# Multiplying C by the scan's running state in three rounded passes, with one more lane step before the state's update (bidirectional SSD encoder, one core)

## The chip, the cores and the metric

The kernel runs on one core of a Trainium2 chip. The metric is device microseconds of one execution, and the kernel before took 1793.29 us, the median of three runs between 1792.80 and 1793.42 us. One more execution was taken with the profiler on; its time and span are in the table below. The profile names the engines PE (matrix multiply), PEld (the load of a matmul's stationary operand), DVE (VectorE), ACT (ScalarE), POOL (GpSimd) and SP (SyncE, which issues the DMAs here).

## The reference

One layer of an encoder is applied to two sequences, a sample of 1024 tokens and a prompt of 256: a normalised row is multiplied by `w_in`, the result goes through three groups of heads (a bidirectional SSD scan, windowed attention, attention to a memory of 256 rows), and the three outputs are multiplied by `w_out` and added to the input. The change lies in the scan. For each chunk of 128 tokens and each direction it is:

```
acs     = cumsum(dt * A)
y_diag  = (C B^T * decay) xdt                  # inside the chunk
states  = B^T (xdt * exp(acs_end - acs))       # what the chunk adds to the state
S_next  = exp(acs_end) * S + states            # running state, 128 x (heads x 64)
y_off   = (C S) * exp(acs)                     # what earlier chunks give: the product of the change
```

Everything is float32.

## The kernel before

**Tiles and blocks.** The 1280 tokens are ten tiles of 128 (`NT`); tiles 0 to 7 are the sample and 8 and 9 the prompt, and they are also two groups of five tiles (640 tokens). The big products run block by block, a block being some columns of a weight: `block_tok` (L234) has tokens as its stationary operand and 512 columns as the moving one, `block_feat` (L269) the other way around, and `block_pair` (L1183) does the first and the last part with sums of weights and rows. Each block runs over the 16 parts k of the inner dimension. A weight is split by `wsplit` (L204) into a rounded high part `h` (ACT copy into float32r, L206) and a remainder `l` (DVE subtraction, L207), the rows are split in the same way, and each product is three passes: high by high, high by low, low by high (L258 to L260, L293 to L295, L1235 to L1237).

**Lanes.** All else (scan, attention, preparation) is written as generators that stand in two queues, `lanes`. Lane 0 has the attention, lane 1 has `dt_prep`, `ssd_up` and `ssd_down`. After each k of a block, `pump` adds the two numbers of `RATES` for that block to what each lane is owed and runs that many steps, alternating between the lanes; a step is the code between two `yield`s. `need` runs a lane on until a named piece is done, at points where a later block reads its result, and in the third `w_out` block, at k = 9, both lanes are emptied at once before their memory is closed. This order is the order of priority; the tile framework places the instructions of each engine from it when the kernel is built, with what it takes to be ready first, and the weight splits are given a higher priority.

**The scan.** `ssd_up(t)` (from L806) goes through the tiles upwards. It turns B and x (L823, L824, L860), and then, for each half g of the 16 heads (512 columns of the running `state`, a 128 x 1024 tile), it multiplies x by the decays and splits the results (`xf`, `fh`, `fl` forward, `xb`, `bh`, `bl` backward), multiplies C by the state (`pyf`, L884, a plain float32 matmul of 128 x 512), scales that into `ya` (L885), multiplies B by the split x in three passes (`pst`, L867 to L869, in `into`), updates the state (L905, L906), and stores the backward contribution `st` (L915, L916). `ssd_down(t)` (from L1014) goes downwards with the stored contributions: `pyb` (L1062) is C by the state, `y` is put together from it (L1064 to L1066), squared (L1069), and then the state is updated (L1071, L1072). Tiles 0 and 8 are `first` and tiles 7 and 9 `last`; `pyf` is made where a tile is not first and `pyb` where it is not last, each for two halves.

**Buffers.** Small tiles come from rings: tag `wb` has four slots of 128 x 512 (`WBB`), tag `bc` and tags `btok` and `btl` one each. The lanes' products go to three PSUM banks (`psum`, tag `mix`), the blocks' sums to five others.

Of the kernel before, what the change touches and what calls it, by code (L numbers as in the profile page):

```python
# [10 lines left out]
F32 = mybir.dt.float32  # L11
F32R = mybir.dt.float32r
# [3 lines left out]
AF = mybir.ActivationFunctionType  # L16
# [3 lines left out]
P = 128  # L20
# [9 lines left out]
RBB = 4  # L30

RATES = ({'kv': (4.0, 1.0), 'z1': (2.2, 1.7)},
         {'kv': (1.4, 1.5), 'x': (2.1, 2.15), 'q': (2.2, 2.5), 'za': (2.1, 2.5), 'z0': (2.1, 2.5),
          'z1': (2.05, 2.55), 'mq': (1.95, 2.7), 'zm': (1.75, 2.75), 'o': (2.1, 2.4)})
FAR = 1e30

UNITS = (0, 8, 1, 9, 2, 10, 3, 11, 4, 12, 5, 13, 6, 7)
# [7 lines left out]
def hymba_encoder_kernel(  # L45
# [7 lines left out]
    V, A, G, T, S = nc.vector, nc.scalar, nc.gpsimd, nc.tensor, nc.sync  # L53
# [72 lines left out]
    def hv(ap, n=8):  # L126
        return ap.rearrange("p (h d) -> p h d", h=n)

    def hb(ap, n, d):
        return ap.unsqueeze(2).broadcast_to([P, n, d])  # L130
# [672 lines left out]
    def wb(name, dtype=F32, shape=(P, 512)):  # L803
        return mp.tile(list(shape), dtype, tag="wb", name=name, bufs=WBB)

    def ssd_up(t):  # L806
        first = t in (0, NS)
        last = t in (NS - 1, NT - 1)
# [12 lines left out]
        ps = psum("pcb")  # L821
# [24 lines left out]
        def rows(q):  # L846

            rf = mp.tile([P, 512], F32, tag="rf", name="rf", bufs=2)
            mt = mp.tile([P, 512], F32, tag="rb", name="rb", bufs=RBB)
            r0 = 32 * (t % 5) + 4 * q  # L850
            for d, r in enumerate((rf, mt)):
                S.dma_start(r, ac_d[t // 5][r0 + 16 * d:r0 + 16 * d + 4, :]
                            .rearrange("h c -> (h c)").partition_broadcast(P))
            rows_[q] = rf, mt

        xsT = []
        for g in range(2):
            ps = psum("pxs")
            for j in range(4):
                T.transpose(ps[:, j * P:(j + 1) * P].bitcast(F32R), xc[g][:, j, :], identr)  # L860
            xt = mp.tile([P, 512], F32, tag="xs", name="xs", bufs=2)
            V.tensor_copy(xt, ps)
            xsT.append(xt)
            yield
        def into(ps, g, h, l):

            T.matmul(ps, bth[:, g, :], h, start=True, stop=False)  # L867
            T.matmul(ps, bth[:, g, :], l, start=False, stop=False)
            T.matmul(ps, btl[:, g, :], h, start=False, stop=True)  # L869

        ya = []
        for g in range(2):
            c = slice(g * 512, (g + 1) * 512)
            a = mp.tile([P, 512], F32, tag="ya", name="ya", bufs=2)
            ya.append(a)
            rows(g)
            if not last:
                xf = wb("xf")
                V.tensor_mul(hv(xf), hv(xsT[g]), hb(dd_all[:, (t + 1) % 6, 8 * g:8 * g + 8], 8, 64))
                fh = wb("fh", F32R)  # L880
                A.activation(fh, xf, AF.Copy)
            if not first:
                pf = psum("pyf")
                T.matmul(pf, bc[:, 2 + g, :], state[:, c], start=True, stop=True)  # L884
                V.tensor_mul(hv(a), hv(pf), hb(eacs_all[:, t, 8 * g:8 * g + 8], 8, 64))  # L885
            yield
            if not last:
                fl = wb("fl", F32R)
                V.tensor_sub(fl, xf, fh.bitcast(F32))
            if not first:  # L890
                xb = wb("xb")
                V.tensor_mul(hv(xb), hv(xsT[g]), hb(dd_all[:, (t + 1) % 6, 16 + 8 * g:24 + 8 * g], 8, 64))
                bh = wb("bh", F32R)
                A.activation(bh, xb, AF.Copy)
            yield
            if not last:
                ps = psum("pst")
                into(ps, g, fh, fl)
                if t == 0 and g == 0:

                    need(mk_prep, range(4))
                if first:
                    V.tensor_copy(state[:, c], ps)
                else:
                    V.tensor_mul(hv(state[:, c]), hv(state[:, c]), hb(cd_all[:, t, 8 * g:8 * g + 8], 8, 64))  # L905
                    V.tensor_add(state[:, c], state[:, c], ps)  # L906
                yield
            if not first:
                bl = wb("bl", F32R)
                V.tensor_sub(bl, xb, bh.bitcast(F32))  # L910
                yield
                ps = psum("pst")
                into(ps, g, bh, bl)
                st = wb("st")
                A.activation(st, ps, AF.Copy)  # L915
                S.dma_start(sb_d[t][:, c], st)  # L916
                yield
# [77 lines left out]
    def norm_ssd():  # L995

        if "y" in last_y:
            t, ys, rs = last_y.pop("y")
            for g in range(2):
                V.tensor_scalar(out=ys[g], in0=ys[g], scalar1=rs[:, g:g + 1], scalar2=None, op0=ALU.mult)  # L1000
                last_y[g] = t, ys[g]
# [12 lines left out]
    def ssd_down(t):  # L1014
        first = t in (0, NS)
        last = t in (NS - 1, NT - 1)
        tok = slice(t * P, (t + 1) * P)
        ss = sm.tile([P, 2], F32, tag="s2", name="yss", bufs=4)
        if not last:
            cc = mp.tile([P, 2, P], F32, tag="btok", name="cc", bufs=1)  # L1020
            S.dma_start(cc, xbc_d[10:12, :, tok].rearrange("f p c -> p f c"))
        ld = []
        for g in range(2):
            c = slice(g * 512, (g + 1) * 512)

            y = mp.tile([P, 512], F32, tag="ya" if t % 2 else "rf", name="yd", bufs=2)
            S.dma_start(y, yp_d[t][:, c])
            if g == 0 and t < 5:
                z = mp.tile([P, 512], F32R, tag="xs", name="zd", bufs=2)
                S.dma_start(hv(z.bitcast(F32), 4), yT_d[:, :, tok])  # L1030
            else:
                z = mp.tile([P, 512], F32, tag="xs", name="zd", bufs=2)
                S.dma_start(z, z_d[g][t])
            st = None
            if not first:
                st = state[:, c] if last else wb("st2")
                S.dma_start(st, sb_d[t][:, c])
            d = mp.tile([P, 4, P], F32R, tag="rb", name="ydT", bufs=RBB)
            S.dma_start(d.bitcast(F32), yd_d[t][:, 4 * g:4 * g + 4, :])
            ld.append((y, z, st, d))  # L1040

        def diag_in(g):
            ps = psum("pd")
            for j in range(4):
                T.transpose(ps[:, j * P:(j + 1) * P].bitcast(F32R), ld[g][3][:, j, :], identr)
            V.tensor_add(ld[g][0], ld[g][0], ps)

        for _ in range(9 if last else 4):
            yield
        norm_ssd()  # L1050
        diag_in(0)
        yield
        for g in range(2):
            c = slice(g * 512, (g + 1) * 512)
            y, z, st, _ = ld[g]
            if g == 0 and t < 5:
                zr, z = z, psum("pz")
                for j in range(4):
                    T.transpose(z[:, j * P:(j + 1) * P].bitcast(F32R), zr[:, j * P:(j + 1) * P], identr)
            if not last:  # L1060
                pf = psum("pyb")
                T.matmul(pf, cc[:, g, :], state[:, c], start=True, stop=True)  # L1062
                y2 = wb("y3")
                V.tensor_mul(hv(y2), hv(pf), hb(eacs_all[:, t, 16 + 8 * g:24 + 8 * g], 8, 64))  # L1064
                V.tensor_add(y, y, y2)
            V.tensor_mul(y, y, z)  # L1066
            if g == 0 and t < 5:
                z = wb("zq")
            A.activation(z, y, AF.Square, scale=0.5, accum_out=ss[:, g:g + 1])  # L1069
            if not first and not last:  # L1070
                V.tensor_mul(hv(state[:, c]), hv(state[:, c]), hb(cd_all[:, t, 16 + 8 * g:24 + 8 * g], 8, 64))  # L1071
                V.tensor_add(state[:, c], state[:, c], st)  # L1072
            yield
            turn_ssd(g)
            if g == 0:
                diag_in(1)
                yield
        rs = sm.tile([P, 2], F32, tag="s2", name="yrs", bufs=4)
        rsqrt(rs, ss, 1.0 / 512, 2)
        G.tensor_scalar(out=rs, in0=rs, scalar1=0.5, scalar2=None, op0=ALU.mult)  # L1080
        last_y["y"] = t, [x[0] for x in ld], rs
        yield
        if first:
            for _ in range(3):
                yield
            norm_ssd()
            yield
            yield
            for g in range(2):
                turn_ssd(g)  # L1090
                yield
# [636 lines left out]
```

## Time and profile before

| | |
|---|---|
| median of three runs | 1793.29 us (1792.80 to 1793.42) |
| the profiled execution: its own time | 1792.72 us |
| the profiled execution: span from first to last instruction | 1791.0 us |
| granted clock of TensorE | 1.000 |
| instructions in the span | 31429 |

The time of an execution is the span and some 1.7 us around it. Stages of the span, from the trace: up to about 580 us the memory block, the first group's blocks in pairs and the preparation; from about 580 to 1200 us the blocks in which `ssd_up` and the attention run beside the second group's products; from 1200 to 1500 us those with `ssd_down`; then the last blocks of `w_out`. A matmul's record has a length that reaches beyond the start of the next one, since matmuls are pipelined: what one costs is read from the distance of starts, not from its length. A matmul whose operands are float32 shows as two records, each with a weight load; one whose operands are float32r shows as one.

### The profile page before, as it was taken

What the parts mean: (1) busy time and instruction counts of PE and PEld (TensorE: products, weight loads), DVE (VectorE), ACT (ScalarE), POOL (GpSimd) and SP (SyncE); (2) the same over time, 40 slices, a digit from 0 to 9 for tenths busy, and PEclk for the clock granted to TensorE, in tenths of its full rate; (3) what the DMA queues carried; (4) which work ended last, traced back from release to release, by engine and by line L of the source; (5) the groups of instructions that cost most, each with busy time, mean ns of one, the idle gap of its engine ahead of it and who ended that gap; (6) DMA issues with size and microseconds to landing.
All of it is one profiled execution on the core that took longest, in us unless ns stands there. A gap on an engine that the chain in (4) does not pass through costs nothing.

```text
span 1791.0 us, 31429 instructions
## 1 busy us (share of the span) xinstructions
PE 1777.5 (99%) x10838; PEld 1605.0 (90%) x10838; DVE 1248.7 (70%) x2358; ACT 922.2 (51%) x2049; POOL 549.6 (31%) x900
## 2 busy tenths in 40 slices
PE   9999999999999999999999999999999999999999
PEld 7789999999998999999889977877988888899999
DVE  5595788888868877778766575557777644766665
ACT  6554555554434766656465565544447533543332
POOL 0105789998810101001001000000100000057775
PEclk9999999999999999999999999999999999999999
DMA  8653444445446644453635645557777754744442
GB/s 292 199 180 114 144 148 149 144 142 163 123 145 207 188 142 137 136 162 111 193 111 179 182 149 162 165 160 249 233 224 238 240 185 149 223 149 144 148 142 77
DMA packets 208207, 301.12 MB, mean 168 GB/s; under 512 B 19568, under 2 KB 86192, under 8 KB 208048
## 3 DMA queue, kind: packets, MB, share of 16 engines
q1 hardware_dynamic: 207904, 299.06, 54.3%
q8 instruction: 85, 1.39, 0.3%
q14 instruction: 74, 0.61, 0.1%
q10 hardware_dynamic: 144, 0.06, 0.0%
HBM read 236.36 MB, written 62.69 MB: 167 GB/s over the span
## 4 chain that ended last, share of the span: by engine, by line
PE 71%; issue 7%; POOL 7%; DVE 6%; DMA 6%; ACT 3%; SPq 0%; POOLq 0%; ACTq 0%; DVEq 0%
PE acc L258 8%; PE acc L260 8%; PE acc L259 8%; PE acc L293 5%; PE acc L1237 5%; PE acc L295 5%; PE acc L294 5%; PE acc L1235 5%; PE acc L1236 5%; POOL ws L1207 4%; PE accm L1236 2%; PE accm L1235 2%; PE accm L1237 2%; POOL wraw L1207 2%; PE po L673 1%
## 5 line engine op out<-in xcount | busy, mean ns | idle before, releaser
L207 DVE TENSOR_TENSOR wl<-wraw,wh 128x512 fp32r<-128x512 f32 (+1 forms) x480 | 345.3, 721 | 220.0 <-ACT wh L206 199.8
L206 ACT ACTIVATE wh<-wraw 128x512 fp32r<-128x512 f32 (+1 forms) x480 | 292.1, 613 | 305.8 <-PE acc L260 154.1
L258 PE MATMUL acc<-wh,xH 128*128 128x512 f32 (+1 forms) x1088 | 418.4, 385 | 0.5 <-ACT mkr L420 0.3
L260 PE MATMUL acc<-wh,xL 128*128 128x512 f32 (+1 forms) x1088 | 411.2, 378 | 0.0
L259 PE MATMUL acc<-wl,xH 128*128 128x512 f32 (+1 forms) x1088 | 410.4, 377 | 0.7 <-DVE wl L207 0.7
L258 PEld LDWEIGHTS acc<-wh,xH 128*128 128x128 f32 x1088 | 204.5, 188 | 38.7 <-issue 3.6
L259 PEld LDWEIGHTS acc<-wl,xH 128*128 128x128 f32 x1088 | 204.6, 188 | 38.2 <-DVE wl L207 3.3
L260 PEld LDWEIGHTS acc<-wh,xL 128*128 128x128 f32 x1088 | 204.4, 188 | 36.8 <-issue 0.6
L293 PE MATMUL acc<-xH,wh 128*128 128x320 f32 x640 | 202.9, 317 | 0.5 <-DVE zs L309 0.5
L206 ACT ACTIVATE sh<-ws 128x384 fp32r<-128x384 f32 x176 | 91.4, 523 | 214.0 <-POOL ws L1207 117.0
L294 PE MATMUL acc<-xL,wh 128*128 128x320 f32 x640 | 199.2, 311 | 0.0
L295 PE MATMUL acc<-xH,wl 128*128 128x320 f32 x640 | 198.3, 310 | 0.0
L207 DVE TENSOR_TENSOR sl<-ws,sh 128x384 fp32r<-128x384 f32 x176 | 124.1, 708 | 105.1 <-ACT sh L206 104.9
L1207 POOL TENSOR_TENSOR ws<-wraw 128x128 f32<-128x128 f32 x176 | 113.5, 645 | 204.5 <-DMA wraw<-in_w_in_pairs_dram 81.1
L635 POOL COPY lg<-nsink 128x2 f32<-128x2 f32 x40 | 16.4, 410 | 373.9 <-PE ppt L663 239.6
L293 PEld LDWEIGHTS acc<-xH,wh 128*128 128x128 f32 x640 | 120.3, 188 | 3.3 <-issue 2.2
L294 PEld LDWEIGHTS acc<-xL,wh 128*128 128x128 f32 x640 | 120.3, 188 | 2.0 <-issue 1.7
L295 PEld LDWEIGHTS acc<-xH,wl 128*128 128x128 f32 x640 | 120.2, 188 | 0.8 <-issue 0.7
L1207 POOL TENSOR_TENSOR ws<-wraw,ws 128x128 f32<-128x128 f32 x176 | 116.6, 662 | 13.8
L1207 POOL TENSOR_TENSOR wraw<-wraw 128x128 f32<-128x128 f32 x176 | 112.2, 638 | 13.7
L1207 POOL TENSOR_TENSOR ws<-ws,wraw 128x128 f32<-128x128 f32 x176 | 115.0, 653 | 0.0
L362 DVE SCALAR_TENSOR_TENSOR c<-u,vec,c 128x638 f32<-128x638 f32 (+1 forms) x96 | 89.7, 936 | 8.9 <-ACT c L357 8.6
(437 smaller groups left out, 3947.0 us busy)
## 6 DMA issues: line engine op xcount, KB each, us to landing
wraw<-in_w_in_laid_dram SPq DMA_DIRECT2D x176, 256.0 KB, 2.9
wraw<-in_w_in_pairs_dram SPq DMA_DIRECT2D x112, 256.0 KB, 2.7
wraw<-in_w_out_laid_dram SPq DMA_DIRECT2D x64, 256.0 KB, 3.0
wraw<-in_w_out_pairs_dram SPq DMA_DIRECT2D x64, 256.0 KB, 2.9
rf<-ac SPq DMA_DIRECT2D x40, 256.0 KB, 4.0
rb<-ac SPq DMA_DIRECT2D x40, 256.0 KB, 4.9
wraw<-in_w_mem_laid_dram SPq DMA_DIRECT2D x32, 256.0 KB, 4.8
xst<-in_x_sample_dram SPq DMA_DIRECT2D x20, 256.0 KB, 4.9
```

The source lines that it names most:

```text
L206: a = A.activation(h, raw, AF.Copy)
L207: b = V.tensor_sub(l, raw, h.bitcast(F32))
L258: T.matmul(ps[t][:, :n], sh, h[:, :n], start=(k_ == 0), stop=False)
L259: T.matmul(ps[t][:, :n], sh, l[:, :n], start=False, stop=False)
L260: T.matmul(ps[t][:, :n], sl, h[:, :n], start=False, stop=(k_ == KT - 1))
L293: T.matmul(o, sh, cur["H", q][:, m, c], start=(k == 0), stop=False)
L294: T.matmul(o, sh, cur["L", q][:, m, c], start=False, stop=False)
L295: T.matmul(o, sl, cur["H", q][:, m, c], start=False, stop=(k == KT - 1))
L1207: G.tensor_tensor(out=o, in0=x, in1=y, op=op)
L1235: T.matmul(ps[p], h, xh, start=(k_ == 0), stop=False)
L1236: T.matmul(ps[p], h, xl, start=False, stop=False)
L1237: T.matmul(ps[p], l, xh, start=False, stop=(k_ == 7))
```

## The change

In `ssd_up`, C (the last two rows of `bc`) is split once for each tile into a high part and a remainder, in place of B, which is no longer needed then. For each half, the state's 512 columns are split into `sh` (ACT) and `sl` (DVE), in two slots of `wb`, in the step in which `xf` and `fh` are made; the product follows a step later, in three float32r passes (`by_state`), with its scaling. Where a tile is neither first nor last, one more `yield` stands before `into`, the product with B that ends in the update of the state. In `ssd_down`, C is split into `cch` and `ccr` (slots `btl` and `btok`), the state's halves into slots of `bc` and `wb`: the first half a step before its product, the second in the step before its own. There the state's update now stands directly behind the product and ahead of the product's scaling, and the square goes into the slot of `y2` instead of a slot of its own. Eight of the lane rates are changed.

```diff
-         {'kv': (1.4, 1.5), 'x': (2.1, 2.15), 'q': (2.2, 2.5), 'za': (2.1, 2.5), 'z0': (2.1, 2.5),
-          'z1': (2.05, 2.55), 'mq': (1.95, 2.7), 'zm': (1.75, 2.75), 'o': (2.1, 2.4)})
+         {'kv': (1.4, 1.5), 'x': (2.1, 2.2), 'q': (2.2, 2.6), 'za': (2.1, 2.65), 'z0': (2.05, 2.65),
+          'z1': (2.0, 2.65), 'mq': (1.95, 2.8), 'zm': (1.75, 2.8), 'o': (2.1, 2.4)})
...
+    def by_state(ps, ch, cl_, h, l):
+
+        T.matmul(ps, ch, h, start=True, stop=False)
+        T.matmul(ps, ch, l, start=False, stop=False)
+        T.matmul(ps, cl_, h, start=False, stop=True)
+
     def ssd_up(t):
...
+        if not first:
+            A.activation(bcr[:, 0:2], bc[:, 2:4], AF.Copy)
+            V.tensor_sub(bcr[:, 2:4], bc[:, 2:4], bc[:, 0:2])
+
         def into(ps, g, h, l):
...
             rows(g)
+            if not first:
+                sh, sl = wb("sh", F32R), wb("sl", F32R)
+                A.activation(sh, state[:, c], AF.Copy)
+                V.tensor_sub(sl, state[:, c], sh.bitcast(F32))
             if not last:
                 xf = wb("xf")
                 V.tensor_mul(hv(xf), hv(xsT[g]), hb(dd_all[:, (t + 1) % 6, 8 * g:8 * g + 8], 8, 64))
                 fh = wb("fh", F32R)
                 A.activation(fh, xf, AF.Copy)
+            yield
             if not first:
                 pf = psum("pyf")
-                T.matmul(pf, bc[:, 2 + g, :], state[:, c], start=True, stop=True)
+                by_state(pf, bcr[:, g, :], bcr[:, 2 + g, :], sh, sl)
                 V.tensor_mul(hv(a), hv(pf), hb(eacs_all[:, t, 8 * g:8 * g + 8], 8, 64))
-            yield
             if not last:
                 fl = wb("fl", F32R)
                 V.tensor_sub(fl, xf, fh.bitcast(F32))
...
             yield
+            if not first and not last:
+                yield
             if not last:
                 ps = psum("pst")
                 into(ps, g, fh, fl)
...
         if not last:
-            cc = mp.tile([P, 2, P], F32, tag="btok", name="cc", bufs=1)
+            ccr = mp.tile([P, 2, P], F32R, tag="btok", name="cc", bufs=1)
+            cc = ccr.bitcast(F32)
             S.dma_start(cc, xbc_d[10:12, :, tok].rearrange("f p c -> p f c"))
...
         norm_ssd()
+        parts = {}
+
+        def halves(g):
+            if last:
+                return
+            c = slice(g * 512, (g + 1) * 512)
+            h = mp.tile([P, 512], F32R, tag="bc", name="sh", bufs=1)
+            l = wb("sl", F32R)
+            A.activation(h, state[:, c], AF.Copy)
+            V.tensor_sub(l, state[:, c], h.bitcast(F32))
+            parts[g] = h, l
+
+        if not last:
+            cch = mp.tile([P, 2, P], F32R, tag="btl", name="cch", bufs=1)
+            A.activation(cch, cc, AF.Copy)
+            V.tensor_sub(ccr, cc, cch.bitcast(F32))
+        halves(0)
         diag_in(0)
         yield
...
             if not last:
                 pf = psum("pyb")
-                T.matmul(pf, cc[:, g, :], state[:, c], start=True, stop=True)
+                by_state(pf, cch[:, g, :], ccr[:, g, :], *parts.pop(g))
+                if not first:
+                    V.tensor_mul(hv(state[:, c]), hv(state[:, c]), hb(cd_all[:, t, 16 + 8 * g:24 + 8 * g], 8, 64))
+                    V.tensor_add(state[:, c], state[:, c], st)
                 y2 = wb("y3")
                 V.tensor_mul(hv(y2), hv(pf), hb(eacs_all[:, t, 16 + 8 * g:24 + 8 * g], 8, 64))
                 V.tensor_add(y, y, y2)
             V.tensor_mul(y, y, z)
             if g == 0 and t < 5:
-                z = wb("zq")
+                z = y2
             A.activation(z, y, AF.Square, scale=0.5, accum_out=ss[:, g:g + 1])
-            if not first and not last:
-                V.tensor_mul(hv(state[:, c]), hv(state[:, c]), hb(cd_all[:, t, 16 + 8 * g:24 + 8 * g], 8, 64))
-                V.tensor_add(state[:, c], state[:, c], st)
             yield
             turn_ssd(g)
             if g == 0:
+                halves(1)
                 diag_in(1)
                 yield
```

## The prediction

> **What bounds the kernel now.** I read the page from the top: busy times, the slices, then the chain that ended last.
>
> ```profile
> span 1791.0 us, 31429 instructions
> PE 1777.5 (99%) x10838; PEld 1605.0 (90%) x10838; DVE 1248.7 (70%) x2358; ACT 922.2 (51%) x2049; POOL 549.6 (31%) x900
> PE   9999999999999999999999999999999999999999
> DVE  5595788888868877778766575557777644766665
> PEclk9999999999999999999999999999999999999999
> PE 71%; issue 7%; POOL 7%; DVE 6%; DMA 6%; ACT 3%; SPq 0%; POOLq 0%; ACTq 0%; DVEq 0%
> ```
>
> TensorE has work in every slice, at full clock, and is without a record for 1791.0 − 1777.5 = 13.5 us. A busy PE need not be an efficient one, so I then asked whom PE waits for, the longest waits first:
>
> ```profile
> PE pmt L767 <- DVE mpr L759: 2.0, 3, 1.1
> PE pyb L1062 <- ACT so L1011: 1.1, 1, 1.1
> PE psc L641 <- DVE nm L643: 0.9, 1, 0.9
> PE acc L259 <- DVE wl L207: 0.7, 3, 0.2
> PE pst L868 <- DVE fl L889: 0.2, 1, 0.2
> ```
>
> No wait of PE is longer than a few us in sum: whatever the lanes do, the instructions placed behind them keep PE fed. So the kernel lasts as long as its matmuls take one after the other, and a change is worth what it takes from that row of matmuls or adds to it, plus new waits in it. The stages of the change, by windows, leave room elsewhere:
>
> ```profile
> 580.00:1200.00 620.00, 616.34 (x3908) 544.83 (x3907) 429.60 (x957) 369.12 (x930) 54.74 (x90) 1.00 0.51 156
> 1200.00:1500.00 300.00, 297.08 (x1700) 249.88 (x1699) 194.16 (x390) 145.54 (x344) 23.25 (x43) 1.00 0.70 218
> ```
>
> The columns after the length are PE, PEld, DVE, ACT and POOL: DVE is busy 69% and 65% of the two stages, ACT 60% and 49%.
>
> **The change part by part.** *The products.* The two old ones, by line, and PE's timeline around one of them, and around a product that already goes in three passes:
>
> ```profile
> L884 PE MATMUL pyf<-state,bc x32: 591/592/697, 645.2 to 1418.9; 128*128 128x512 f32 x32
> L1062 PE MATMUL pyb<-state,cc x32: 590/593/697, 1203.0 to 1500.1; 128*128 128x512 f32 x32
> 645.20 1.02 PE L884 MATMUL pyf<-state,bc 128*128 128x512 f32 x2
> 646.05 0.60 PE L663 MATMUL ppt<-identr,lg 128*128 128x128 f32 x4
> 648.36 0.40 PE L867 MATMUL pst<-fh,bth 128*128 128x512 f32 x1
> 648.59 0.40 PE L868 MATMUL pst<-fl,bth 128*128 128x512 f32 x1
> 648.82 0.39 PE L869 MATMUL pst<-fh,btl 128*128 128x512 f32 x1
> 649.05 0.31 PE L294 MATMUL acc<-xL,wh 128*128 128x320 f32 x1
> ```
>
> Each line has 32 records, two to a product: 16 products in `ssd_up` (tiles 1 to 7 and 9, two halves) and 16 in `ssd_down`, 32 in all. The records' lengths (0.59 us) overlap and say little; the starts say what a product costs: from 645.20 to the next matmul at 646.05 it is 0.85 us in plain float32. Three float32r passes of the same 128x512 shape start 0.23 us apart and give PE on from 648.36 to 649.05, 0.69 us. `by_state` has that shape and that type, so each product becomes 0.16 us shorter, and 32 of them take 32 × 0.16 = 5.1 us out of the row of matmuls. PE has nothing to hide this in, so it counts in full.
>
> A page weighs in here. The Trainium skill (FP8 and Floating Point Precision, TensorE Precision Notes) says that true FP32 is four passes through the array. By that an old product would take 4 × 0.23 = 0.92 us and the gain be 32 × 0.23 = 7.4 us; the trace has 0.85 us, 3.7 passes, and I go by the trace.
>
> *The splits.* Each product now needs its half of the state copied by ACT and subtracted by DVE, and each tile its C. Rows of the same kinds:
>
> ```profile
> L881 ACT ACTIVATE fh<-xf 128x512 fp32r<-128x512 f32 x16 | 10.0, 626 | 13.7 <-DVE xf L879 11.1 <-DMA rb<-ac 2.6
> L889 DVE TENSOR_TENSOR fl<-xf,fh 128x512 fp32r<-128x512 f32 x16 | 11.0, 689 | 5.1 <-ACT fh L881 5.0
> L617 ACT ACTIVATE qh<-q 128x256 fp32r<-128x256 f32 x20 | 7.8, 408 | 8.2 <-DVE q L611 8.2
> L618 DVE TENSOR_TENSOR qh<-q,qh 128x256 fp32r<-128x256 f32 x20 | 8.1, 419 | 1.0 <-ACT qh L617 1.0
> ```
>
> ACT gets 32 × 0.626 + 16 × 0.408 = 26.6 us, DVE 32 × 0.689 + 16 × 0.419 = 28.7 us. In the two stages DVE goes from 429.6 + 194.2 = 624 to 653 of 920 us, 71%, and ACT from 515 to 541. What hides them is the block's matmuls on PE; if that cover were gone, one split would cost its full 0.626 + 0.689 = 1.3 us, 42 us for all 32.
>
> *The new wait.* The product now waits for `sl`, which is made one lane step earlier. Behind it on PE stand the block's matmuls, and for those wait the block's evacuations and all else. No row shows this wait, but `pst` has the same one, for `fl`, and over its 32 products it cost PE 0.2 us in one place (above). The bounds are 0 (PE is handed a product only when it is ready) and 42 us (each split exposed); I take 0.2 us, the row that is like it in every respect but the lane's distance.
>
> *More work on DVE and ACT.* PE's waits for DVE and ACT in the rows above come to 4.9 us. If they grow as DVE's work in these stages does, 28.7 / 624 = 4.6%, that is 0.2 us; some rows are not shown, so I put 0.4. Bounds: a loss of as much again as the waits that are there, 5 us, and a gain of the 1.1 us at `pyb`, since other instructions will stand before it.
>
> *The state's update ahead of the scaling.* In `ssd_down`, for the 12 halves that have an update, two DVE instructions now stand ahead of the one that reads `pf`:
>
> ```profile
> L1071 DVE TENSOR_TENSOR state<-state,cd_all x12: 680/681/685, 1205.0 to 1308.8; 128x512 f32<-128x512 f32 x12
> L1072 DVE TENSOR_TENSOR state<-state,st x12: 681/686/690, 1206.2 to 1310.0; 128x512 f32<-128x512 f32 x12
>   ACT so L1011: 2.8, 3
> ```
>
> They need the halves split, not the product, so they can run before PE is done, and then cost nothing. At worst they hold one of three PSUM banks 0.681 + 0.686 = 1.37 us longer; the last row is what `pyb` waited for in its old place, mostly such a bank (2.8 us in three places, by the view of its line, which counts the weight load's waits too). I take 0.
>
> *Lane steps and rates.* One `yield` more for each half of tiles 1 to 6 makes 12 more steps of lane 1; from its yields, `ssd_up(2)` goes from 36 steps to 38. Counting both kernels' steps against their rates, block by block, the pieces end where they did within some k: `ssd_up(7)` at k = 14 of block z1 instead of 13, `ssd_down(7)` starts at k = 0 of mq in both, `ssd_down(0)`, which a later block needs, ends at k = 1 of the first `w_out` block in both, and when the lanes are emptied 3 steps are left instead of 5. No `need` forces a step in either. So I cost this at 0; what hides it is the distance from `ssd_down(0)` to its reader, one whole block, and if that were used up, `w_out` would wait. No DMA is added, and SP's and POOL's queues keep their order. Using `y2` for the square frees a slot and adds no wait, since the square waits for `y` anyway.
>
> *The sum.* −5.1 + 0.2 + 0.4 = −4.5 us. The profiled execution took 1792.72 us (its span and 1.7 us around it) and becomes 1788.2; it is 0.57 us below the median, so by the median the forecast is 1793.3 − 4.5 = **1788.8 us**, 0.25% faster. About 0.2%, 3.6 us, is what a measurement of this kernel can tell from no change, so faster begins below 1789.7 us.
>
> **The rivals.** *The bank takes it back.* If the banks are held 1.37 us longer in 12 places and PE waits for it in as many as it now waits for `so`, 3 of them, 4.1 us are lost: −4.5 + 4.1, so 1792.9 us, no change that can be told. For it speaks that three banks serve all lane products; against it that the update can run ahead of the product.
>
> *The ring of four.* This one ends on the other side. In `ssd_up`, `sh` and `sl` are drawn from `wb` ahead of `xf` and `fh`, four slots at once, and for the second half one of the four still holds the `st` of the first half, on its way out to memory:
>
> ```profile
> sb<-st SPq DMA_DIRECT2D x16, 256.0 KB, 3.3
> ```
>
> Before, only `xf` and `fh` were drawn at that point. If `fh` has to wait for the landing, 3.3 us, less the 0.63 + 0.69 us of the split ahead of it, ACT stands 2.0 us with the block's weight splits queued behind it, in six places (tiles 1 to 6). If all of it came through to PE it would be 6 × 2.0 = 12 us, hence 1788.8 + 12.0 = 1800.8 us. It makes the kernel slower (by over 0.2%) from 8.1 / 6 = 1.35 us a place. Against it: the weights are split ahead of their use (`wl` held PE only 0.7 us), and a framework that knows of the slot can put other ACT work first.
>
> *More than the bare passes.* If the 1.1 us of `pyb` and the 2.0 us that PE waits at `pmt` go in the new order, 1788.8 − 3.1 = 1785.7 us. The new order may also move such waits instead.
>
> *The weight loads are the bound.* A product has three loads instead of two, 32 more:
>
> ```profile
> L884 PEld LDWEIGHTS pyf<-state,bc x32: 186/189/193, 645.1 to 1418.5; 128*128 128x128 f32 x32
> 642.85 0.19 PEld L293 LDWEIGHTS acc<-xH,wh 128*128 128x128 f32 x1
> 643.00 0.19 PEld L294 LDWEIGHTS acc<-xL,wh 128*128 128x128 f32 x1
> ```
>
> If PE's time went with their number, 32 × 0.189 = 6.0 us would be added and the kernel take 1793.3 + 6.0 = 1799.3 us. But loads of 0.19 us start 0.15 us apart, beside matmuls, and three of them lie within the 0.69 us of a `pst`: they are hidden. The Trainium skill (Perfetto Trace Analysis, Identifying the Most-Contended Engine) says that matmul busy time is a bad measure of headroom and that the share of LDWEIGHTS is the good one. By that rule this change, which raises the share, goes the wrong way; the trace speaks against it here, and I leave it a small chance.
>
> *It does not do what it says.* If float32r passes from these tiles ran at the plain float32 pace, three would cost more, not less; every float32r row here is at 0.23 us, so this has no chance of its own.
>
> **How the numbers follow.** The forecast has 0.47, the bank 0.25, the ring 0.16, more than the passes 0.10, the loads 0.02. The forecast's own range is 1787.0 to 1790.5 us (the waits from 0 to some 2 us more, the passes measured to 0.01 us each), and nine tenths of it, 0.42, lie below 1789.7. Faster: 0.42 + 0.10 = 0.52. Same: 0.05 + 0.25 = 0.30. Slower: 0.16 + 0.02 = 0.18. The range leaves out the ring and the loads, and so reaches from 1785.0, below the case of more than the passes, to 1794.0, above the bank's 1792.9.
>
> **What would show it.** In the changed trace `by_state` has 96 records, 0.23 us apart, 0.69 us to the next matmul; if the distance is over 0.8, the first step is wrong. PE's waits for `sl` and `ccr` stay under 1 us; several us there mean that the split is too late. DVE rises by about 29 and ACT by about 27 us. A wait of ACT `fh` for the store of `st`, with later `wh` behind it, would show the ring, and more or longer waits at `pyb`, `pd`, `psc` or `pmt` the bank. What would make the forecast wrong is most of all the order of instructions: it is worked out anew for the changed kernel, and moves PE's few us of waits by as much as the gain.

## The result, and the profile after

The changed kernel takes 1797.86 us (median of ten runs, 1795.73 to 1800.88) beside 1793.34 us of the kernel before (ten runs, 1790.97 to 1794.36): 0.27% slower, ratio 1.0027 with a 95% interval of 1.0018 to 1.0036. The forecast was 1788.8 us. The profiled execution took 1795.89 us, 3.2 us more than the one of before, so it shows some two thirds of the difference.

The page after, its span and its busy times:

```profile
span 1794.2 us, 31591 instructions
PE 1775.1 (99%) x10870; PEld 1611.3 (90%) x10870; DVE 1272.5 (71%) x2406; ACT 943.4 (53%) x2097; POOL 554.4 (31%) x900
```

PE is busy 2.4 us less, yet the span is 3.2 us longer: its time without a record went from 13.5 to 19.1 us. So PE got less to do and lost more than that by waiting. First the part that came as forecast, PE's timeline of the changed kernel around one of the new products:

```profile
644.86 0.48 PE L808 MATMUL pyf<-sh,bc 128*128 128x512 f32 x1
645.18 0.40 PE L809 MATMUL pyf<-sl,bc 128*128 128x512 f32 x1
645.41 0.39 PE L810 MATMUL pyf<-sh,bc 128*128 128x512 f32 x1
645.64 0.28 PE L641 MATMUL psc<-kT,qT 128*128 128x256 f32 x1
```

From the second pass on they stand 0.23 us apart. The first record is long (0.48 us) because it starts inside the transposes before it; what a matmul costs is the distance of its end from the end of the one before, for the third pass here 645.80 − 645.58 = 0.22 us. The median of these distances over all records is 0.43 us for each of the two records of an old product, 0.859 us in all, and 0.23 us for a pass, 0.697 us for three. For 32 products that is 5.2 us less work for PE, where the forecast had 5.1. If each of the 10838 (now 10870) records is put down at the median of its kind (same target, same shape), the sum goes from 1761 to 1756 us. What the distances exceed these medians by went from 24 to 32 us.

Then the waits of PE, longest first (total, times, longest):

```profile
PE pxs L866 <- ACT mpr L754: 2.1, 1, 2.1
PE acc L259 <- DVE wl L207: 1.8, 4, 1.1
PE psc L641 <- ACT qT L625: 1.7, 2, 1.5
PE warm L1546 <- DVE zero L1544: 1.3, 1, 1.3
PE acc L258 <- DVE zs L319: 1.0, 1, 1.0
PE pz L1093 <- DVE nm L643: 1.0, 1, 1.0
PE pmt L767 <- DVE mpr L759: 1.0, 3, 0.6
PE pyf L808 <- ACT sh L889: 0.9, 1, 0.9
PE acc L258 <- DVE yt L410: 0.9, 1, 0.9
PE pyb L808 <- ACT so L1027: 0.7, 1, 0.7
PE acc L1272 <- DVE wl L207: 0.7, 1, 0.7
PE acc L258 <- DVE v_all L337: 0.6, 2, 0.3
PE pst L878 <- DVE bl L926: 0.5, 1, 0.5
PE psc L641 <- ACT pT L664: 0.2, 1, 0.2
```

All rows of this list together come to 14.4 us, those of before to 9.0. Of the 14.4, 1.3 us is the start (`warm`), as before; the five rows at the blocks' own matmuls (`acc`) have 5.0 us, before 2.5; the products of the lanes have 8.1, before 5.2. Only one of these waits, 0.9 us at `pyf`, is for a split of the change. The others are for instructions that were there before. At the lanes' products PE needs a bank that ACT or DVE has not read yet (`pxs`, `pz`, `pyb`) or an operand that they have yet to make (`qT`, `mpr`, `bl`); at the blocks' matmuls it needs the remainder of a weight (`wl`) or a bank (`zs`, `yt`, `v_all`).

Where in the span is it lost? The blocks' matmuls are the same 8880 in both kernels and in the same order, so the time at which the same one ends can be compared in the two profiled executions, from a common point at 500 us:

| end of block matmul number (time before) | 6480 (1310 us) | 6960 (1447 us) | 7200 (1514 us) | 7680 (1611 us) and the end |
|---|---|---|---|---|
| changed kernel minus before | −2.8 us | +1.3 us | +0.9 us | +3.7 us |

Up to 1310 us the change is 2.8 us ahead. It then loses 4.1 us in the last `zm` block and the first blocks of `w_out`, where `ssd_down(0)`, `ssd_up(8)`, the memory attention and the row fills for the next blocks meet, and 2.8 us more after the lanes are empty, where the change adds no instruction.

### The profile page after: what moved, and what is told of

Same layout as the page of the kernel before. It is cut to its first block, busy times and chain, and to the rows that moved or that the text cites. A ratio compares the mean times of both kernels' runs of the same rounds, so it can differ in the third digit from the quotient of the medians.

```text
span 1794.2 us, 31591 instructions
## 1 busy us (share of the span) xinstructions
PE 1775.1 (99%) x10870; PEld 1611.3 (90%) x10870; DVE 1272.5 (71%) x2406; ACT 943.4 (53%) x2097; POOL 554.4 (31%) x900
## 4 chain that ended last, share of the span: by engine, by line
PE 49%; DVE 3%; DMA 3%; ACT 2%; issue 1%; POOL 1%; SPq 0%; POOLq 0%; DVEq 0%; ACTq 0%
PE acc L258 7%; PE acc L260 7%; PE acc L259 7%; PE acc L293 3%; PE acc L295 3%; PE acc L294 3%; PE acc L1272 3%; PE acc L1271 3%; PE acc L1270 3%; PE po L673 1%; PE ppt L663 1%; PE accm L1272 1%; PE accm L1271 1%; PE accm L1270 1%; PE py L957 1%
```

## Experiments

Every kernel was timed against the kernel before on the same chip, in five rounds; the ratio is to that kernel, whose median in these groups of runs was 1791.8 to 1792.5 us. One profiled execution can be some us off the median of its kernel (5.3 us for `e4_passes_only`, 3.9 us for `e13_fill_pool`), so the verdicts go by the ratios, and a trace tells where its one execution waited.

**Parts, rates, and the bare passes.** My theory was that the passes gain as forecast and the downward part gives back more; the rivals were the rates, and any new order of instructions. `e1_up_only` is the changed kernel with the whole of `ssd_down` as it was before:

> The changed kernel with ssd_down put back as it was before, so that only ssd_up's 16 products go in three passes; the new rates stay. Theory (the passes gain some 4.5 us as forecast, and the downward part of the change gives back more than that): 1790 to 1792 us beside 1793.3, about 2 us faster, since half of the passes' gain is left and the loss is not. Rival 1 (the rates cost it): slower than before, 1796 or more. Rival 2 (any new order of the instructions costs PE a few us of waits, whichever part it comes from): 1794 to 1797.

Measured: 1799.34 us, ratio 1.0042 (1.0029 to 1.0055), the worst of the parts. `e2_down_only` is the kernel before with the changed `ssd_down` alone:

> The kernel before with the changed ssd_down alone; ssd_up and the rates are as before. Theory (the downward part loses): 1797 to 1800 us, 4 to 7 us slower than before. Rival 1 (the rates): about 1791, 2.3 us faster. Rival 2 (any new order): 1794 to 1797.

Measured: 1793.23 us, 1.0004 (0.9995 to 1.0012). My theory falls with these two, as the downward part is not what costs, and neither rival's range holds the second. `e3_rates_only`:

```diff
-         {'kv': (1.4, 1.5), 'x': (2.1, 2.15), 'q': (2.2, 2.5), 'za': (2.1, 2.5), 'z0': (2.1, 2.5),
-          'z1': (2.05, 2.55), 'mq': (1.95, 2.7), 'zm': (1.75, 2.75), 'o': (2.1, 2.4)})
+         {'kv': (1.4, 1.5), 'x': (2.1, 2.2), 'q': (2.2, 2.6), 'za': (2.1, 2.65), 'z0': (2.05, 2.65),
+          'z1': (2.0, 2.65), 'mq': (1.95, 2.8), 'zm': (1.75, 2.8), 'o': (2.1, 2.4)})
```

> The kernel before with the new rates and nothing else: no instruction is added, the lanes' steps fall in other places. Theory (the downward part): 1792.5 to 1794.5, within 1 us of before. Rival 1 (the rates cost it): 1797 or more. Rival 2 (any new order costs): 1794 to 1797, without any product changed.

Measured: 1797.12 us, 1.0033 (1.0022 to 1.0044): rates that add no instruction cost as much as the whole change. `e4_passes_only`:

```diff
-                T.matmul(pf, bc[:, 2 + g, :], state[:, c], start=True, stop=True)
+                for i in range(3):
+                    T.matmul(pf, bth[:, g, :], state_r[:, c], start=(i == 0), stop=(i == 2))
...
-                T.matmul(pf, cc[:, g, :], state[:, c], start=True, stop=True)
+                for i in range(3):
+                    T.matmul(pf, identr, state_r[:, c], start=(i == 0), stop=(i == 2))
...
```

This kernel leaves out the splits and multiplies by whatever rounded operand is at hand, so it does not compute the layer.

> The kernel before with each of the 32 products as three float32r passes of the state, which is kept rounded, by an operand that is rounded already (B turned, the identity): no split, no added step, the old rates; four copies of a loaded state into place are added on DVE. Computed is another product, so only the time counts. Theory (the passes gain): 5 us faster than before, 1788 to 1789. If the passes do not gain what the distances of starts say, it is at 1793 or more, and if any new order costs, at 1790 to 1792.

Measured: 1789.95 us, 0.9986 (0.9976 to 0.9996), 2.5 us faster (0.7 to 4.3), which is between the theory's range and that of any new order. The passes gain, but only about half of the 5.2 us reaches the end, with no split, step or rate added (four copies on DVE are). A reading that fits is that PE comes sooner to the places where it has to wait for the lanes' ACT and DVE chains; its one trace, of the slowest of its twelve executions, cannot show it.

**Which rates, and is it any new order?** `e9_rate_nudge`:

```diff
-         {'kv': (1.4, 1.5), 'x': (2.1, 2.15), 'q': (2.2, 2.5), 'za': (2.1, 2.5), 'z0': (2.1, 2.5),
+         {'kv': (1.4, 1.5), 'x': (2.1, 2.14), 'q': (2.2, 2.5), 'za': (2.1, 2.5), 'z0': (2.1, 2.5),
```

> The kernel before with one number changed, lane 1's rate in the x blocks from 2.15 to 2.14, which moves a few steps of the scan by one k and adds nothing. Theory 1 (the new rates are bad because they run lane 1 faster): within 1 us of before. Theory 2 (every new order costs): 1794.5 to 1798, 2 us or more above before.

Measured: 1792.42 us, 1.0001 (0.9991 to 1.0010). "Any new order costs" falls in this plain form. `e10_late_rates`:

```diff
-          'z1': (2.05, 2.55), 'mq': (1.95, 2.7), 'zm': (1.75, 2.75), 'o': (2.1, 2.4)})
+          'z1': (2.05, 2.55), 'mq': (1.95, 2.8), 'zm': (1.75, 2.8), 'o': (2.1, 2.4)})
```

> The kernel before with the new rates in the blocks mq and zm only, where ssd_down runs. Theory 1 (the rates, in the blocks where they differ most from what the lane needs): since the trace of the rates alone lost 3.5 of its 4.6 us after 1180 us, some 3 us above before. Theory 2: 1794.5 to 1798 as well, but the loss shows where the order differs, and not more in these blocks than the nudge loses elsewhere.

Measured: 1795.71 us, 1.0027 (1.0017 to 1.0037), by the ratio 4.8 us and by the medians 3.4: two rates hold most of what the eight cost. In its trace PE has a wait, the first row here, that the kernel before does not have, and the changed kernel does:

```profile
PE pxs L860 <- ACT mpr L754: 3.0, 1, 3.0
PE pmt L767 <- DVE mpr L759: 2.1, 2, 1.1
```

ACT's timeline at this place tells why, of the changed kernel first, then of `e10_late_rates`, then of the kernel before (start, length, instruction; rows between are left out in the last two):

```profile
1340.56 0.83 ACT L200 ACTIVATE xH<-chd,vec 128x640 fp32r<-128x640 f32 x1 [4.43 <-DMA chd<-oT]
1341.30 0.62 ACT L206 ACTIVATE wh<-wraw 128x512 fp32r<-128x512 f32 x1
1341.82 2.25 ACT L200 ACTIVATE xH<-chd,vec 128x640 fp32r<-128x640 f32 x3
1343.98 0.55 ACT L754 ACTIVATE mpr<-pms,mm,mr 128x256 f32<-128x256 f32 x1
```

```profile
1345.40 2.25 ACT L200 ACTIVATE xH<-chd,vec 128x640 fp32r<-128x640 f32 x3
1347.55 0.55 ACT L754 ACTIVATE mpr<-pms,mm,mr 128x256 f32<-128x256 f32 x1
```

```profile
1343.24 0.56 ACT L754 ACTIVATE mpr<-pms,mm,mr 128x256 f32<-128x256 f32 x1 [1.84 <-DVE mm L750]
1344.60 0.57 ACT L754 ACTIVATE mpr<-pms,mm,mr 128x256 f32<-128x256 f32 x1
1346.32 1.67 ACT L200 ACTIVATE xH<-chd,vec 128x640 fp32r<-128x640 f32 x2 [0.51 <-DMA chd<-oT]
```

`mpr` reads the bank that PE needs for `pxs`. In the changed kernel and in `e10_late_rates` three fills of rows (L200, `chd` from the scan's output, 2.25 us) stand ahead of it on ACT; in the kernel before they come after it. The fills wait for `ssd_down(0)`, which ends earlier with the faster lane. Counting the lanes' steps again showed that `ssd_down(0)` is forced at k = 1 of the first `w_out` block, by 3 steps before and by 1 with the new rates.

**The fills.** `e12_late_two_steps` is `e10_late_rates` with two empty steps in `ssd_down(0)`, so that 3 steps are forced again:

```diff
-            for _ in range(3):
+            for _ in range(5 if t == 0 else 3):
```

> The kernel before with the new rates in mq and zm, which alone made it 3.4 us slower, and the two empty steps in ssd_down(0). No split anywhere. Theory (placement of the fills): back to within 1 us of before, 1792 to 1793.5, without the wait at pxs. Rival (the rates cost through ssd_down's denser steps, before the fills): still 3 us or more above before.

Measured: 1793.00 us, 1.0008 (0.9999 to 1.0017), and its list of PE's waits has no `pxs`. Two empty steps take back most of what the late rates cost the kernel before (1.0027 to 1.0008), so there they cost through where `ssd_down(0)` ends and the fills start. `e11_two_steps` makes the same edit in the changed kernel:

> The changed kernel with two empty steps more near the end of ssd_down(0), so that it ends at the same step of the first w_out block as in the kernel before (3 steps forced there instead of 1), and with it the row fills that wait for it. Theory (placement: with the faster lane these fills come some us earlier and stand on ACT ahead of the readers of the PSUM banks that PE needs next): the 2.3 us wait at pxs goes, and some of the 4.6 us that the changed kernel loses between 1310 and 1446 us: 1794 to 1796, 2 to 4 us below the changed kernel. Rival (the splits' work on DVE and ACT keeps PE waiting, wherever the fills stand): within 1 us of the changed kernel.

Measured: 1797.93 us, 1.0030 (1.0018 to 1.0042). The wait at `pxs` is gone here too, and nothing is gained: its trace has 1.2 us at `pms`, where the changed kernel has none, and others later. `e14_refill_later`:

```diff
-        tok("o", w_out_rows(c), ev_out(c * 512), None if c else refill_o(0, {1: 2, 5: 3}), grp=1)
+        tok("o", w_out_rows(c), ev_out(c * 512), None if c else refill_o(0, {2: 2, 6: 3}), grp=1)
```

> The changed kernel with the row fills of the last two quads asked for one k later in the first w_out block (k = 2 and 6 instead of 1 and 5). Theory (placement of the fills): the wait at pxs goes or moves, 1794 to 1796.5. Rival (splits' work): within 1 us of the changed kernel, or slower if the fills are then late for the next block.

Measured: 1796.75 us, 1.0022 (1.0013 to 1.0030); the wait at `pxs` for `mpr` stays, at 1.5 us. `e13_fill_pool`:

```diff
-            A.activation(h, ch, AF.Copy, scale=gain)
+            if tc_fill[0]:
+                G.tensor_scalar(out=h, in0=ch, scalar1=gain, scalar2=None, op0=ALU.mult)
+            else:
+                A.activation(h, ch, AF.Copy, scale=gain)
...
+    tc_fill[0] = True
     for c in range(2):
```

> The changed kernel with the high part of those fills made on POOL, which has little to do there, instead of ACT. Theory (the fills stand on ACT ahead of the readers of the banks): pxs waits for ACT no more, 1794 to 1796.5, unless POOL is so slow with a 128x640 tile that the fills themselves are late. Rival (splits' work on DVE and ACT): 0.82 us less on ACT for each of 8 fills changes little, within 1 us of the changed kernel.

Measured: 1799.22 us, 1.0045 (1.0031 to 1.0059): POOL's records for such a tile are 2.0 us long, DVE waits 5.7 us for it, and PE's wait at `pxs` grows to 4.3 us. So in the changed kernel moving the fills brought nothing, and they are not the cause by themselves.

**Rates and update in the changed kernel.** `e6_old_rates` puts the rates back (the reverse of the diff of `e3_rates_only`):

> The changed kernel with the eight rates put back. Theory 1 (the rates cost some 4.6 us by themselves and add to the rest): 1793 us, 4.6 us below the changed kernel. Theory 2 (every new order costs PE a few us of waits, and the rates are only one way to a new order): 1795 to 1799, no clear gain from putting them back, since this is a new order as well.

Measured: 1797.80 us, 1.0029 (1.0020 to 1.0038), no gain. With the old rates the 12 added steps leave 10 steps of `ssd_down(0)` to be forced, so the old rates do not bring the old order back. `e5_update_behind`:

```diff
                 by_state(pf, cch[:, g, :], ccr[:, g, :], *parts.pop(g))
-                if not first:
-                    V.tensor_mul(hv(state[:, c]), hv(state[:, c]), hb(cd_all[:, t, 16 + 8 * g:24 + 8 * g], 8, 64))
-                    V.tensor_add(state[:, c], state[:, c], st)
...
             A.activation(z, y, AF.Square, scale=0.5, accum_out=ss[:, g:g + 1])
+            if not first and not last:
+                V.tensor_mul(hv(state[:, c]), hv(state[:, c]), hb(cd_all[:, t, 16 + 8 * g:24 + 8 * g], 8, 64))
+                V.tensor_add(state[:, c], state[:, c], st)
```

> The changed kernel with the state's update in ssd_down behind the square again, as it was before. If the update ahead of the scaling holds the PSUM bank of pyb longer (the bank rival of the forecast): up to 4 us below the changed kernel. Theory 1 (rates): within 1 us of the changed kernel. Theory 2 (every new order): anywhere between 1795 and 1800.

Measured: 1796.80 us, 1.0030 (1.0019 to 1.0042), no gain either.

**Splits or steps?** `e15_steps_rates` is the changed kernel without the splits of the state and of C:

```diff
...
-                sh, sl = wb("sh", F32R), wb("sl", F32R)
...
-                by_state(pf, bcr[:, g, :], bcr[:, 2 + g, :], sh, sl)
+                T.matmul(pf, bc[:, 2 + g, :], state[:, c], start=True, stop=True)
...
-                by_state(pf, cch[:, g, :], ccr[:, g, :], *parts.pop(g))
+                T.matmul(pf, cc[:, g, :], state[:, c], start=True, stop=True)
```

> The changed kernel without any split and with the plain float32 products: left are its lane steps (product a step later, one step more ahead of the update), its rates, the update ahead of the scaling and the slot of y2. Theory A (placement: what the steps and rates move costs most of the added waits): 1796 to 1799, 4 to 6 us above before, so that the splits cost no more than the passes gain. Theory B (the splits' work and latency cost most of it): 1792 to 1795.

Measured: 1792.74 us, 1.0005 (0.9996 to 1.0014). Theory A falls: without splits the steps and rates together cost 0.9 us, which cannot be told from nothing. Yet its trace has the fills ahead of `mpr` too, and a longer wait than the changed kernel's:

```profile
PE pxs L866 <- ACT mpr L754: 2.9, 1, 2.9
```

So a kernel can have this wait and be no slower than the one before, as far as can be told. Compared as in the table of the result, this execution stands at −2.7, +2.0, +1.9 and +2.0 us at the four places: with no split in it, it loses 4.7 us between 1310 and 1447 us, no less than the changed kernel, and nothing after 1514 us. Beside it, in these two executions, the changed kernel's shorter products have not put it ahead by 1310 us, and it alone loses after the lanes are empty. `e7_splits_plain` keeps the splits and takes the passes away:

```diff
-        T.matmul(ps, ch, h, start=True, stop=False)
-        T.matmul(ps, ch, l, start=False, stop=False)
-        T.matmul(ps, cl_, h, start=False, stop=True)
+        T.matmul(ps, ch.bitcast(F32), h.bitcast(F32), start=True, stop=True)
```

> The changed kernel with all its splits, steps and rates, but one plain float32 product of the high parts in place of three passes; the low parts are made and not used, so the product is a rounded one. If the passes gain their 5.2 us in full in this setting: 1802 to 1804. If PE, once faster, only waits longer at the same places (the waits are set by ACT and DVE, not by PE): within 2 us of the changed kernel, 1796 to 1800.

Measured: 1797.65 us, 1.0031 (1.0020 to 1.0042). So at these steps and rates the splits cost 0.0031 − 0.0005, 4.7 us with an uncertainty of some 2.5, and the passes' 5.2 us do not reach the end: 1.0031 without them, 1.0027 with them. `e16_up_no_step` is `e1_up_only` with the old rates and without the step ahead of `into`:

> The kernel before with ssd_up's splits and passes (16 products) and the product a step later, without the one step more ahead of the update, with ssd_down and the rates as before: no step count changes. Theory A (placement): since no step moves, close to what the passes gain, 1790 to 1793. Theory B (splits): 1795 to 1798, as the part in ssd_up is what the runs so far cannot clear.

Measured: 1792.95 us, 1.0005 (0.9996 to 1.0014), against 1.0042 for the up part with step and new rates, and within the range of theory A. `e17_down_behind` is `e2_down_only` with the update behind the square:

> The kernel before with the changed ssd_down, its update behind the square as before, and ssd_up and the rates as before: the 16 products of ssd_down in passes, no step and no order of the update changed. Theory A: the down part alone was 0.7 us above before with the update ahead; without that 1790.5 to 1793. If the update ahead was a help, 1793 to 1795. A kernel that beats the one before would most likely be this one.

Measured: 1790.47 us, 0.9991 (0.9982 to 0.9999). It is the one version with the true products that is faster than the kernel before, by 1.5 us, with an interval that just leaves out no change; among so many kernels one may come out so by chance. The row of the longest wait at a lane's product in its trace, and one of the next ones:

```profile
PE pmt L767 <- DVE mpr L759: 1.9, 3, 1.0
PE psc L641 <- DVE nm L643: 0.8, 1, 0.8
```

**All 32 products, part by part.** `e18_both_behind` joins `e16_up_no_step` and `e17_down_behind`; `e19_both_ahead` has the update ahead of the scaling as the change has it:

> All 32 products in passes with their splits, the product a step later, but without the step ahead of the update, with the old rates and with the update in ssd_down behind the square: the up part that cost 1.0 us by itself and the down part that gained 1.5 us. If the parts add: 1791 to 1792, 0.5 us below before. If the waits grow with the splits' total load on ACT and DVE, wherever the steps stand: 1795 to 1798, as in the changed kernel.

Measured: 1792.38 us, 1.0004 (0.9995 to 1.0013), close to the parts added and well below the other range.

> The same with the update in ssd_down ahead of the scaling, as the change has it; against the changed kernel with old rates (5.3 us above before) only the 12 added steps are missing. If the added steps make the difference: 1792 to 1794. If the place of the update does, 2 us above the kernel with the update behind, as it was for the down part alone (0.7 above before against 1.5 below). If neither does but the splits' load: 1796 to 1798.

Measured: 1794.47 us, 1.0015 (1.0006 to 1.0024). With `e4_passes_only`, `e6_old_rates` and the changed kernel these make a ladder, each beside the kernel before (ratio times 1792 us):

| kernel | beside before | step |
|---|---|---|
| bare passes (`e4_passes_only`) | −2.5 us | −2.5 us |
| with splits, product a step later (`e18_both_behind`) | +0.7 us | +3.2 us |
| with the update ahead (`e19_both_ahead`) | +2.7 us | +2.0 us |
| with the 12 steps (`e6_old_rates`) | +5.2 us | +2.5 us |
| with the rates (changed kernel) | +4.8 us | −0.4 us |

The first step has an uncertainty of 1.8 us, each of the others of some 2.3 us (two intervals of 1.6 us or more together), so the first is shown, the second and fourth lie just outside it, and the last is none. For the third the two kernels ran on one chip in the same rounds, eleven times each, and their medians are 2.1 us apart. The update's place comes out at 2 us twice: here, and in the down part alone (1.0004 ahead, 0.9991 behind).

## Why the prediction was wrong

**The work of PE: right; "it counts in full": wrong.** PE's row of matmuls became 5.2 us shorter by the distances of their ends, forecast 5.1. But the bare passes brought 2.5 us of it to the end, and in the changed kernel's own setting the passes brought 0.7 (`e7_splits_plain` to the changed kernel), which cannot be told from nothing. The Trainium skill's four passes for true FP32 (FP8 and Floating Point Precision, TensorE Precision Notes) would, at the pace of a float32r pass, have made it 7.4 us. The medians stay with 0.859 / 0.232 = 3.7 such passes. That does not count the passes: if there are four, each would take less time than a float32r pass here.

**The splits' size: right.** By line:

```profile
L889 ACT ACTIVATE sh<-state 128x512 fp32r<-128x512 f32 x16 | 10.0, 624 | 0.0
L1076 ACT ACTIVATE sh<-state 128x512 fp32r<-128x512 f32 x16 | 10.0, 625 | 4.4 <-PE pyb L810 4.3
L890 DVE TENSOR_TENSOR sl<-state,sh 128x512 fp32r<-128x512 f32 x16 | 11.0, 687 | 3.8 <-ACT sh L889 3.7
L1077 DVE TENSOR_TENSOR sl<-state,sh 128x512 fp32r<-128x512 f32 x16 | 11.0, 686 | 0.1
```

With the splits of C that is 26.6 us on ACT and 28.7 us on DVE, as put down; the busy times on the page rise by less, 21.2 and 23.8 us, since records that overlap count once there. PE waited directly for a state split once, for 0.9 us, so "the new wait" of 0.2 us was mis-sized by less than a microsecond. The row of L1076 shows a wait that the prediction did not name: in five places, 4.3 us in all, a split in `ssd_down` waits for an earlier product, which by the code still reads the one slot of `bc`. The runs do not price it, but `e17_down_behind` has 8.7 us of it and is the fastest kernel with the true products.

**"More work on DVE and ACT", 0.4 us: this step failed.** It scaled PE's existing waits by the 4.6% that DVE's work grows. The waits do not scale so. At the changed kernel's own steps and rates the splits cost 4.7 us (`e15_steps_rates` to `e7_splits_plain`, the lists of PE's waits 8.3 and 12.6 us), and on the bare passes 3.2 us with the product a step later, where the forecast had 0.6 for both terms of the splits. In that setting the account is +0.9 us for steps and rates, +4.7 for the splits and −0.7 for the passes, 4.8 us in all. The upper bound that the prediction gave this term, 5 us, would have held it. How the splits come to cost this much is read from the lists of waits and not shown for each place: PE's waits for ACT and DVE went from 9.0 to 14.4 us, nearly half of the growth at the blocks' own matmuls, where a remainder `wl` or the reading of a bank comes later. The reading that fits is that such places are set by chains of work on ACT and DVE, so that a PE with less to do waits there longer, and more instructions on ACT and DVE move them back.

**"The state's update ahead of the scaling", 0: mis-sized, as far as two pairs of kernels go.** Its price as a rival was 4.1 us; the two pairs have it at about 2. That a held bank is the reason was not shown, and in the full change putting it back brought nothing (1.0030 beside 1.0027).

**"Lane steps and rates", 0: wrong in its reason.** The text said that the reader of `ssd_down(0)` is a whole block away and that nothing is forced. The row fills of the first `w_out` block ask for it at k = 1 and k = 5, so it is forced there in both kernels. It is 3 steps before and 1 in the changed kernel. In the kernel before, the late rates by themselves cost 3.4 us by the medians (4.8 by the ratio), and two empty steps took most of it back. Together with the added steps and the update ahead, the eight rates cost 0.9 us (`e15_steps_rates`), so in the full change the 0 was off by little.

**The rivals.** The ring of four did not show itself: in the trace of the changed kernel `fh` waits for `xf` and for no store. The bound by weight loads would have given 1799.3 us, near what was measured, and the rule of the Trainium skill (Perfetto Trace Analysis, Identifying the Most-Contended Engine), which beside the share of LDWEIGHTS names one more measure, points that way. But it is not the reason: the bare passes have the same 32 loads more and are faster than before.

**What stays open.** The parts do not add. Down alone −1.5, up alone +1.0 and both together +0.7 us do so within their intervals. But the up part with step and rates costs 7.5 us, steps and rates without splits 0.9, and taking the rates, the update's place or the fills back out of the full change brought at most 1 us. The instructions are placed anew for each kernel, and which waits of ACT and DVE fall together then is not something that these runs reduce to one cause. The prediction's last sentence named this order as what would most likely make it wrong, and gave it no term in the sum. The last stage shows how far it goes: after 1514 us, where the lanes have run empty and the code of all these kernels is the same, the profiled executions of the changed kernel, `e11_two_steps` and `e15_steps_rates` lose 2.8, 4.7 and 0.1 us.

## What to carry to other kernels

When PE is 99% busy, saved PE time still has to pass the places where PE waits for a chain on other engines. Look for these with the list of waits and with ACT's timeline around them, and do not count a saving there in full. In the kernel here about half of a bare saving came through, and it was less than what two further instructions for each product on busy neighbours then cost. Where such costs come from the order of instructions, a kernel that leaves out one part at a time prices them better than the waits of one trace: the same 2 to 3 us wait at `pxs` stood in a kernel that was slower and in one that was not. Before a rate, a step or an order is costed at nothing, find who reads its result, and check the code for the place where it is asked for.

## What the runs showed of the hardware that was not expected

By the profile POOL took 2.01 us to scale a 128x640 tile into float32r, where ACT took 0.83 us (L200, above):

```profile
L203 POOL TENSOR_SCALAR xH<-chd,vec 128x640 fp32r<-128x640 f32 x8 | 16.0, 2012 | 23.1 <-DMA chd<-oT 23.1
```
